# Attention's probabilities times values: native fp32 operands instead of rounded high and low halves

## The chip, the cores and the metric

The kernel runs on one core of a Trainium2 chip. The core has five engines that the text names: TensorE (in the profile PE, with its weight loads as PEld), VectorE (DVE), ScalarE (ACT), GpSimd (POOL) and SyncE (SP), which issues the transfers. Each works through its own queue in the order in which the program was laid out, and waits on semaphores for the others. The metric is the device time of one execution in microseconds (us), lower is better.

## The reference

The reference computes two layers of a diffusion backbone on 512 latent tokens and 256 context tokens of width 1024. Layer 0 mixes tokens by pooling, layer 1 by attention with 8 query heads and 2 key/value heads of width 128; each is followed by an MLP of width 4096 with squared ReLU. The change touches layer 1's attention alone:

```python
def attend(q, k, v):
    s = jnp.einsum('bqhgd,bkhd->bhgqk', q, k).astype(jnp.float32) * (HEAD_DIM ** -0.5)
    p = jax.nn.softmax(s, axis=-1).astype(v.dtype)
    return jnp.einsum('bhgqk,bkhd->bqhgd', p, v)
```

Queries are the 512 latent tokens; keys and values are all 768 tokens. Everything is fp32. The attention output is then multiplied by `w_o` (1024 x 1024).

## The kernel before

**Halves.** Most matmuls take fp32 operands as two rounded halves. ScalarE writes `hi`, the fp32 number rounded to the type that the listing calls `F32R` (fp32r in the profile); VectorE writes `lo = x - hi`, also as fp32r; and TensorE adds three products: hi x hi, hi x lo, lo x hi. A few matmuls (adaLN vectors at L226, gate rows at L302, pooling means at L420) take fp32 operands directly.

**Attention, tile by tile.** A step `i` is a pair (head h, query tile t of 128 tokens); there are 8 x 4 = 32. `s_scores` (L1183) makes 128 x 768 scores with six matmuls (L1191) into one of two large PSUM buffers, VectorE takes the row maximum (L1195), ScalarE the exponential with its row sum (L1196) into a buffer `p` of 768 columns, `pbuf(i % 4)`. `s_norm` (L1200) takes the reciprocal of the row sum (L1202) and scales `p` in place: on VectorE (L1204) in 17 of the steps, on ScalarE (L1206) in 15, by a table written out in the code. `s_turn` (L1208) turns the six 128 x 128 blocks of `p` on TensorE (L1216), three at a time into a PSUM tile `pspt`; ScalarE casts each to the high half (L1218), VectorE subtracts for the low half (L1219). `s_values` (L1221) runs once for two query tiles: for each of six key tiles three matmuls with 128 value columns as weights and 256 queries streaming (L1230), then the output `po` is split into `oH` and `oL` (L1232, L1233). `q_head` (L1175) turns a head's queries (L1179) and splits them.

**Before the attention.** `kv_a` to `kv_c` project keys and values for six token tiles. `kv_e` splits the values into `vH` (L1076) and `vL` (L1077); `kv_b` writes the normalised and rotated keys into a work row `kf`, `kv_c` turns them (L1090). `q_a` projects the queries (L1018) with weight blocks that lie in `unit[0]`, `unit[1]` and `unit[2]`.

**Where things lie.** `unit[1]` and `unit[2]` are two areas of 4096 fp32r columns in one allocation. During the attention the turned probabilities take 3072 columns of each (`pTL`, `pTH`), and the query halves of heads 2 to 7 the rest. Afterwards the second half of the output weights (`wo[1]`) is split into them, in quarters of 512 columns (`split`, L125; L128 and L131).

**Order.** Every piece of work has a time in a list (`st.at`), and the pieces are issued sorted by it; a planner that simulates the program then fixes the order in each engine's queue, save for instructions that are pinned to program order. `attention` (L1271) gives step i its times in units of 2.7 from a base: scores at i + 0.2, scaling at i + 1.3, turning at i + 3.1, values at i + 5.2 for odd t. The output projection (`attn_mm`, L1256) follows in eight blocks; the third is the first that reads `wo[1]`. A tile area that is given back to its pool can be used again when all readers and writers of the old tile are through.

Of the kernel before, what the change touches and what calls it, by code (L numbers as in the profile page):

```python
# [9 lines left out]
F32 = mybir.dt.float32  # L10
F32R = mybir.dt.float32r
BF16 = mybir.dt.bfloat16
AF = mybir.ActivationFunctionType
ALU = mybir.AluOpType
# [3 lines left out]
P = 128  # L18
D = 1024
KT = D // P  # L20
LAT = 512
CTX = 256
TOK = LAT + CTX
NL = LAT // P
NT = TOK // P
# [17 lines left out]
class Steps:  # L43
# [3 lines left out]
    def at(self, t, fn, *args):  # L47
        self.items.append((t, len(self.items), fn, args))
# [7 lines left out]
def backbone(ctx: ExitStack, tc, x, c, ctx_in, c_ctx, w_ada, b_ada, g_mix_pre, g_mix_post,  # L56
# [3 lines left out]
    sy, ve, sc, gp, te = nc.sync, nc.vector, nc.scalar, nc.gpsimd, nc.tensor  # L60
# [3 lines left out]
    rawp = ctx.enter_context(tc.tile_pool(name="rawp", bufs=3, side="right"))  # L64
# [5 lines left out]
    def residents(stack):  # L70
        pool = stack.enter_context(tc.tile_pool(name="residents", bufs=1, side="right"))
        return (pool.tile([P, NT, D], F32, name="xr"), pool.tile([P, 2, D], F32, name="gate"),
                pool.tile([P, D], BF16, name="junk"))

    xr, gate, junk = residents(held[0])
# [4 lines left out]
    acc = const.tile([P, NT * D], F32, name="acc")  # L80
# [9 lines left out]
    ra = const.tile([P, 2 * KT * TOK], F32R, name="ra")  # L90
    rb = const.tile([P, 10240], F32R, name="rb")
    phase = ctx.enter_context(tc.tile_pool(name="phase", bufs=1)).tile([P, 40], F32, name="phase")
    rawe = ExitStack()
    pools = [rawe.enter_context(tc.tile_pool(name="rawe", bufs=4))]
    unit, pinned = [rb[:, 6144:10240]], [True]

    def open_units():
        rawe.close()
        pools[0] = rawp
        units = ctx.enter_context(tc.tile_pool(name="units", bufs=1)).tile([P, 2 * 4096], F32R, name="units")  # L100
        unit.extend(units[:, 4096 * i: 4096 * (i + 1)] for i in range(2))
    minus = phase[:, 0:2 * KT].rearrange("p (k c) -> p k c", c=2)
    hH = ra[:, 0:KT * TOK].rearrange("p (k n) -> p k n", n=TOK)
    hL = ra[:, KT * TOK:].rearrange("p (k n) -> p k n", n=TOK)
# [2 lines left out]
    def raw_load(src, pool=None):  # L107
        t = (pool or pools[0]).tile([P, 2048], F32, tag="raw", name="raw")
        d = sy.dma_start(t, src)
        if pinned[0]:  # L110
            tc.keep_in_program_order(d)
        return t
# [7 lines left out]
    def split_halves(raw, hi, lo, pin=False):  # L120
        for q in range(2):
            z = slice(1024 * q, 1024 * q + 1024)
            split(raw[:, z], hi[:, z], lo[:, z], pin)
# [13 lines left out]
    class Ring:  # L137
# [1 line left out]
            self.slots, self.n, self.halves = slots, 0, halves  # L139

        def load(self, src, width, pin=False, wait=None):
            raw = raw_load(src, rawp)
            s = self.slots[self.n % len(self.slots)]
            self.n += 1
            hi, lo = s[:, 0:2048], s[:, 2048:4096]
            if wait is None and self.halves:
                split_halves(raw, hi, lo, pin)
            elif wait is None:
                split(raw, hi, lo, pin)
            else:  # L150
                wait.append((raw, hi, lo))
            f = lambda a: a.rearrange("p (k n) -> p k n", n=width)
            return f(hi), f(lo)
# [559 lines left out]
    st = Steps()  # L713
# [13 lines left out]
    raws = []  # L727
# [6 lines left out]
    for n, t in enumerate(order):  # L734
        b = 55 + 3 * n
# [9 lines left out]
    for (t, q), z in block.items():  # L745
        st.at(z, turn0, t, q)
        st.at(z + 0.8, mod0, t, q)
        for f in range(2):
            st.at(z + 2.4 if q < 3 else 83 + 2 * f + t / 10, parts0, t, q, f)
    st.at(200, open_units)  # L750
    st.run()

    pso = {}
# [230 lines left out]

    kTH = rb[:, 0:1536].rearrange("p (h n) -> p h n", n=TOK)
    kTL = rb[:, 1536:3072].rearrange("p (h n) -> p h n", n=TOK)
    vH = rb[:, 3072:4608].rearrange("p (t n) -> p t n", n=256)
    vL = rb[:, 4608:6144].rearrange("p (t n) -> p t n", n=256)
    q32 = acc[:, 0:NL * D].rearrange("p (t n) -> p t n", n=D)
    tabs = acc[:, 4 * D:6 * D].rearrange("p (w s t n) -> p w s t n", w=2, s=2, t=NL)  # L990
    swap = lambda a, o: a.rearrange("p (h o d) -> p h o d", o=2, d=32)[:, :, o, :]
# [72 lines left out]
    def norm_g(t, pool=False, cols=HALVES):  # L1064
        yg[t] = work_tile()
        for c0, w in cols:
            z = gated(t, yg[t], accv[:, t, c0:c0 + w], c0, c0 + w, pool)
            if cols == THIRDS:
                tc.keep_in_program_order(z)

    def kv_a(t):
        pj[t] = project(t, chunks[2])

    def kv_e(t):
        ps = pj[t]
        sc.copy(vH[:, t, :], ps[:, 256:512])  # L1076
        ve.tensor_tensor(out=vL[:, t, :], in0=ps[:, 256:512], in1=vH[:, t, :], op=ALU.subtract)  # L1077
        pj[t] = ps, head_rstd(ps, NKV)

    def kv_b(t):  # L1080
        ps, r = pj[t]
        kf = xr[:, 4, 256 * (t % 4):256 * (t % 4) + 256]
        head_norm(ps, r, NKV, 1, t, kf)
        pj[t] = kf

# [59 lines left out]
    def before0():  # L1145
# [8 lines left out]
        for t in (4, 5, 0, 1, 2, 3):  # L1154
# [3 lines left out]

    oH = ra[:, 0:4096].rearrange("p (h n) -> p h n", n=LAT)
    oL = ra[:, 4096:8192].rearrange("p (h n) -> p h n", n=LAT)  # L1160
    qTs = [(z[:, 0:512], z[:, 512:1024]) for z in (unit[0][:, 0:1024], unit[0][:, 1024:2048],
                                                    unit[1][:, 3072:4096], unit[2][:, 3072:4096])]
    qbuf = lambda h: qTs[h if h < 2 else 2 + h % 2]
    pTH = unit[2][:, 0:NT * LAT].rearrange("p (s n) -> p s n", n=LAT)
    pTL = unit[1][:, 0:NT * LAT].rearrange("p (s n) -> p s n", n=LAT)
    pbuf = lambda i: (xr[:, 4, 0:TOK], xr[:, 5, 0:TOK], gate[:, 1, 0:TOK], acc[:, 4 * D:4 * D + TOK])[i]
    aring = Ring([ra[:, 8192:12288], unit[0], unit[1], unit[2]])

    def wo_unit(ch, kk, wait=None):
        return aring.load(w_o[ch, kk], 512, True, wait)  # L1170
# [29 lines left out]
    def s_norm(i):  # L1200
        sm, p = smx[i], pbuf(i % 4)
        ve.reciprocal(sm[:, 2:3], sm[:, 1:2])  # L1202
        if (False,False,False,True,False,True,True,True,True,True,True,True,False,False,True,False,True,False,True,False,True,True,True,False,False,True,False,False,False,False,True,True)[i]:
            ve.tensor_scalar(out=p, in0=p, scalar1=sm[:, 2:3], scalar2=None, op0=ALU.mult)  # L1204
        else:
            sc.activation(p, p, AF.Copy, scale=sm[:, 2:3])  # L1206

    def s_turn(i):  # L1208
        _, t = steps[i]
        sl = slice(t * P, (t + 1) * P)  # L1210
        p = pbuf(i % 4)
        for b in range(2):
            ps = psB.tile([P, 3, P], F32, tag="b", name="pspt")
            for j in range(3):
                k = 3 * b + j
                te.transpose(ps[:, j, :], p[:, k * P:(k + 1) * P], ident)  # L1216
            hi, lo = pTH[:, 3 * b:3 * b + 3, sl], pTL[:, 3 * b:3 * b + 3, sl]
            sc.copy(hi, ps)  # L1218
            ve.tensor_tensor(out=lo, in0=ps, in1=hi, op=ALU.subtract)  # L1219

    def s_values(i):  # L1221
        h, t = steps[i]
        half = t // 2
        kv = h // 4
        hs = slice(kv * HD, (kv + 1) * HD)
        qs = slice(256 * half, 256 * half + 256)
        po = psB.tile([P, 512], F32, tag="b", name="po")
        for kt in range(NT):
            for n, (v, p) in enumerate(((vH, pTH), (vL, pTH), (vH, pTL))):
                te.matmul(po[:, 0:256], v[:, kt, hs], p[:, kt, qs],  # L1230
                          start=(kt == 0 and n == 0), stop=(kt == NT - 1 and n == 2))
        sc.copy(oH[:, h, qs], po[:, 0:256])  # L1232
        ve.tensor_tensor(out=oL[:, h, qs], in0=po[:, 0:256], in1=oH[:, h, qs], op=ALU.subtract)  # L1233

    wo = {0: [], 1: []}
# [35 lines left out]
    def attention(st, base, unit_t):  # L1271
        at = lambda i, fn, *args: st.at(base + unit_t * i, fn, *args)
        for i, (h, t) in enumerate(steps):
            if t == 0:
                at([-2, 3, 4.542, 7.928, 13.236, 15.602, 19.752, 23.755][h], q_head, h)
            at(i + 0.2, s_scores, i)
            at(i + 1.3, s_norm, i)
            at(i + 3.1, s_turn, i)
            if t % 2:
                at(i + 5.2, s_values, i)  # L1280
        raws = []
        at(7, lambda: wo[0].append(wo_unit(0, 0, raws)))
        at(11.386, lambda: wo[0].append(wo_unit(0, 1, raws)))
        for n in range(8):
            at(9.05 + 2 * n, lambda n: split(*raws[n // 4], True, n % 4), n)
        for kk in range(2):
            at((23.386, 25.741)[kk], lambda kk: wo[1].append(wo_unit(1, kk, raws)), kk)
        at(37.812, lambda: split(*raws[2], q=0))
        at(38.427, lambda: split(*raws[2], q=1))
        at(37.814, lambda: split(*raws[2], q=2))  # L1290
        at(37.815, lambda: split(*raws[2], q=3))
        at(39.191, lambda: split(*raws[3], q=0))
        at(39.192, lambda: split(*raws[3], q=1))
        at(39.193, lambda: split(*raws[3], q=2))
        at(45.691, lambda: split(*raws[3], q=3))
        at(39.281, gate_diag if False else gate_rows, 1, GT1, 0)
# [118 lines left out]
```

## Time and profile before

| | us |
|---|---|
| median of three runs (lowest, highest) | 1178.87 (1178.73, 1179.42) |
| the profiled execution's own time | 1180.54 |
| its span, first to last instruction | 1178.7 |
| PE busy in the span | 1142.6 |
| VectorE busy | 941.9 |
| ScalarE busy | 637.5 |
| attention's scores, first matmul to last value matmul | 680.6 to 787.2 |

A group row of the profile reads: line, engine, operation, output and input tiles, shapes and count; then busy time and the mean duration of one in ns; then the engine's idle time just before these instructions and what ended it. A row of the timeline or of the chain begins with the start and the length in us. Durations of matmuls overlap: the spacing of a run of them is its length, less the last one's duration, divided by one less than their count. All profile numbers come from one execution.

### The profile page before, as it was taken

To read this page: it belongs to the slowest core of one execution; us is meant where nothing else is said; L and a number is where in the kernel's file an instruction comes from. 1 tells how busy PE (TensorE), PEld (TensorE's weight loads), DVE (VectorE), ACT (ScalarE), POOL (GpSimd) and SP (SyncE) were. 2 spreads that over 40 slices of the span, in tenths; PEclk is the share of its full clock that TensorE was granted. 3 is DMA by queue.
4 is the path that set the end of the run, shared out by engine and by line. 5 is a ranking of instruction groups with operands and counts; after the bars stand their busy time and mean duration, and the time that the engine had idled before them with its cause. 6 is when DMAs were issued, how large, how long until landed. Compare 5 with 4: busy or idle time off the path is not lost.

```text
span 1178.7 us, 15984 instructions
## 1 busy us (share of the span) xinstructions
PE 1142.6 (97%) x6170; PEld 989.5 (84%) x6170; DVE 941.9 (80%) x1546; ACT 637.5 (54%) x1087; POOL 67.2 (6%) x120
## 2 busy tenths in 40 slices
PE   5899999999999999999999999999899999999997
PEld 4679888989889988998887889998888888888886
DVE  3786778998988999896787689877687779778876
ACT  3666654555354445554676377863676346535522
POOL 2030000000000000000141210001100000000001
PEclk9899999999999999999999999999999999999999
DMA  8974222333334334334422101115234124304312
GB/s 325 369 290 196 72 72 107 143 143 144 143 143 142 113 139 143 107 132 151 182 72 75 70 1 36 37 43 199 110 119 174 48 97 142 108 36 143 107 38 105
DMA packets 25642, 147.84 MB, mean 125 GB/s; under 512 B 2736, under 2 KB 5216, under 8 KB 9824
## 3 DMA queue, kind: packets, MB, share of 16 engines
q1 hardware_dynamic: 25568, 146.84, 34.1%
q8 instruction: 48, 0.79, 0.3%
q14 instruction: 26, 0.21, 0.1%
HBM read 139.49 MB, written 7.34 MB: 125 GB/s over the span
## 4 chain that ended last, share of the span: by engine, by line
PE 54%; issue 33%; DVE 5%; ACT 3%; POOL 3%; DMA 1%; SPq 0%; POOLq 0%; DVEq 0%; ACTq 0%
PE pso L771 22%; PE psin L677 18%; PE psin L553 3%; PE po L1230 2%; PE psy L1256 2%; PE psq L1018 2%; PE pss L1191 2%; POOL rs L171 1%; PE psada L226 1%; PE psm L420 1%; POOL rs L1027 1%; ACT junk L156 1%; DVE sm L1195 1%; PE pspt L1216 1%; DVE units L1219 1%
## 5 line engine op out<-in xcount | busy, mean ns | idle before, releaser
L771 PE MATMUL pso<-units,rb 128*128 128x512 f32 x1152 | 278.9, 392 | 0.0
L771 PEld LDWEIGHTS pso<-units,rb 128*128 128x128 f32 x1152 | 214.7, 188 | 41.1
L268 DVE SCALAR_TENSOR_TENSOR rows<-raw,cond,rows 128x256 f32<-128x256 f32 x280 | 127.1, 479 | 2.0
L783 DVE TENSOR_TENSOR acc<-acc,pso 128x512 f32<-128x512 f32 x129 | 85.4, 677 | 41.8 <-PE pso L771 41.7
L553 PE MATMUL psin<-ra,rb 128*128 128x512 f32 (+1 forms) x432 | 104.8, 342 | 2.4 <-ACT ra L363 1.6
L875 PE MATMUL pso<-units,pairs 128*128 128x512 f32 x336 | 82.3, 389 | 0.0
L553 PEld LDWEIGHTS psin<-ra,rb 128*128 128x128 f32 x432 | 70.3, 189 | 13.7 <-ACT ra L363 1.9
L553 PE MATMUL psin<-ra 128*128 128x512 f32 x256 | 80.5, 389 | 0.0
L875 PEld LDWEIGHTS pso<-units,pairs 128*128 128x128 f32 x336 | 63.1, 188 | 13.1
L879 DVE TENSOR_TENSOR acc<-acc,pso 128x512 f32<-128x512 f32 x72 | 48.8, 683 | 28.6 <-PE pso L875 28.6
L169 POOL TENSOR_SCALAR ms<-ss 128x1 f32<-128x1 f32 x20 | 11.0, 549 | 1000.7 <-ACT junk L156 989.2
L677 PE MATMUL psin<-ra,units 128*128 128x384 f32 x336 | 65.5, 337 | 0.4 <-ACT psin L689 0.4
L677 PE MATMUL psin<-sums,units 128*128 128x384 f32 x336 | 64.0, 336 | 0.0
L677 PEld LDWEIGHTS psin<-ra,units 128*128 128x128 f32 x336 | 59.8, 188 | 3.9 <-ACT psin L689 0.5
L131 DVE TENSOR_TENSOR units<-raw,units 128x1024 fp32r<-128x1024 f32 (+2 forms) x49 | 55.2, 1153 | 6.5 <-ACT units L128 6.3
L677 PEld LDWEIGHTS psin<-sums,units 128*128 128x128 f32 x336 | 58.9, 188 | 1.6
L128 ACT CAST units<-raw 128x1024 fp32r<-128x1024 f32 (+2 forms) x49 | 46.9, 995 | 17.7 <-PE pso L771 13.7
L553 PEld LDWEIGHTS psin<-ra 128*128 128x128 f32 x256 | 48.1, 188 | 10.0
L781 ACT COPY acc<-pso 128x512 f32<-128x512 f32 x48 | 27.1, 587 | 48.2 <-PE pso L771 47.7
L553 PE MATMUL psin<-rb 128*128 128x512 f32 (+1 forms) x144 | 52.8, 367 | 0.2 <-DVE rb L364 0.2
L1018 PE MATMUL psq<-units,ra 128*128 128x512 f32 x216 | 51.7, 392 | 0.0
L553 PE MATMUL psin<-rb,ra 128*128 128x512 f32 x128 | 49.8, 389 | 0.0
(255 smaller groups left out, 2355.7 us busy)
## 6 DMA issues: line engine op xcount, KB each, us to landing
raw<-in_w_ada SPq DMA_DIRECT2D x48, 1024.0 KB, 4.9
raw<-in_w_mlp_in SPq DMA_DIRECT2D x32, 1024.0 KB, 4.8
raw<-in_w_mlp_out SPq DMA_DIRECT2D x32, 1024.0 KB, 5.0
raw<-in_w_qkv SPq DMA_DIRECT2D x6, 1024.0 KB, 4.8
spill<-xr SPq DMA_DIRECT2D x10, 512.0 KB, 9.1
xr<-spill SPq DMA_DIRECT2D x10, 512.0 KB, 5.6
raw<-in_w_o SPq DMA_DIRECT2D x4, 1024.0 KB, 4.9
xr<-in_x SPq DMA_DIRECT2D x4, 512.0 KB, 4.4
```

The costliest lines, as they stand in the source:

```text
L128: a = sc.copy(hi, raw)
L131: b = ve.tensor_tensor(out=lo, in0=raw, in1=hi, op=ALU.subtract)
L268: ve.scalar_tensor_tensor(out=r, in0=raw[:, k, :], scalar=cond[:, k, c:c + 1], in1=r, op0=ALU.mult, op1=ALU.add)
L553: te.matmul(ps[:, bank, o:o + ln], w[:, k, fs], rhs, start=start, stop=(k == KT - 1 and n == 2), skip_group_check=len(ks) < KT)
L677: te.matmul(bank, w[k], a[k], start=start and k == 0 and m == 0, stop=stop and k == 3 and m == 2, skip_group_check=True)
L771: te.matmul(pss[h][:, 0:cols[h][1]], a[:, f, ts_], w[:, f, cols[h][0]:sum(cols[h])], start=(n == 0 and not seeded[t]), stop=(n == len(seq) ...
L781: sc.copy(d, ps)
L783: ve.tensor_tensor(out=d, in0=d, in1=ps[:, 0:w], op=ALU.add)
L875: te.matmul(ps, a, w, start=(m == 0), stop=(m == len(seq) - 1))
L879: ve.tensor_tensor(out=M[n][:, t], in0=M[n][:, t], in1=ps, op=ALU.add)
L1018: te.matmul(ps, a[:, k, sl], w[:, k % 4, :], start=(k == 0 and n == 0), stop=(k == KT - 1 and n == 2))
L1191: te.matmul(ps[:, c2, 0:384], a[:, sl], b[:, kv, 384 * c2:384 * c2 + 384], start=(n == 0), stop=(n == 2))
```

## The change

- `s_values` multiplies fp32 probabilities by fp32 values: one matmul per key tile instead of three.
- The turned probabilities are copied once, as fp32 (`soft["t"]`), and the values are copied once, as fp32 (`values()`, in the rows 4 and 5 of `xr`, which are free by then); L1077 and L1219 are gone.
- The keys' work row `kf` has two places instead of four.
- All 32 scalings are on VectorE.
- `unit[1]` and `unit[2]` are given up at the start of the attention (`open_soft`) for fp32 tiles: query halves of heads 2 to 7, turned probabilities, two of the four `p` buffers. At the end (`close_soft`) the two units are opened again. The second half of `w_o` is loaded at the same steps as before, but gets its place in a unit after that.

```diff
     def open_units():
-        rawe.close()
-        pools[0] = rawp
-        units = ctx.enter_context(tc.tile_pool(name="units", bufs=1)).tile([P, 2 * 4096], F32R, name="units")
-        unit.extend(units[:, 4096 * i: 4096 * (i + 1)] for i in range(2))
+        units = uheld[0].enter_context(tc.tile_pool(name="units", bufs=1)).tile([P, 2 * 4096], F32R, name="units")
+        unit[1:] = [units[:, 4096 * i: 4096 * (i + 1)] for i in range(2)]
...
+    values = lambda: xr[:, 4:6].rearrange("p t n -> p (t n)")[:, 0:1536].rearrange("p (t n) -> p t n", n=256)
...
-        sc.copy(vH[:, t, :], ps[:, 256:512])
-        ve.tensor_tensor(out=vL[:, t, :], in0=ps[:, 256:512], in1=vH[:, t, :], op=ALU.subtract)
+        sc.copy(values()[:, t, :], ps[:, 256:512])
...
-        kf = xr[:, 4, 256 * (t % 4):256 * (t % 4) + 256]
+        kf = xr[:, 5, 512 + 256 * (t % 2):768 + 256 * (t % 2)]
...
-    pbuf = lambda i: (xr[:, 4, 0:TOK], xr[:, 5, 0:TOK], gate[:, 1, 0:TOK], acc[:, 4 * D:4 * D + TOK])[i]
-    aring = Ring([ra[:, 8192:12288], unit[0], unit[1], unit[2]])
+    aring = Ring([ra[:, 8192:12288], unit[0], None, None])
+    soft = {}
+
+    def open_soft():
+        uheld[0].close()
+        pool = uheld[0].enter_context(tc.tile_pool(name="soft", bufs=1))
+        qs = pool.tile([P, 2 * 1024], F32R, name="qs")
+        qTs.extend((qs[:, 1024 * i:1024 * i + 512], qs[:, 1024 * i + 512:1024 * i + 1024]) for i in range(2))
+        soft["t"] = pool.tile([P, NT, LAT], F32, name="pT")
+        ps = [pool.tile([P, TOK], F32, name=f"p{i}") for i in range(2)]
+        soft["p"] = ps
+
+    def close_soft():
+        uheld[0].close()
+        open_units()
+        aring.slots[2:] = unit[1:]
+
+    pbuf = lambda i: soft["p"][i - 1] if i in (1, 2) else (gate[:, 1, 0:TOK], acc[:, 4 * D:4 * D + TOK])[i // 2]
...
-        if (False,False,False,True,False,True,True,True,True,True,True,True,False,False,True,False,True,False,True,False,True,True,True,False,False,True,False,False,False,False,True,True)[i]:
-            ve.tensor_scalar(out=p, in0=p, scalar1=sm[:, 2:3], scalar2=None, op0=ALU.mult)
-        else:
-            sc.activation(p, p, AF.Copy, scale=sm[:, 2:3])
+        ve.tensor_scalar(out=p, in0=p, scalar1=sm[:, 2:3], scalar2=None, op0=ALU.mult)
...
-            hi, lo = pTH[:, 3 * b:3 * b + 3, sl], pTL[:, 3 * b:3 * b + 3, sl]
-            sc.copy(hi, ps)
-            ve.tensor_tensor(out=lo, in0=ps, in1=hi, op=ALU.subtract)
+            sc.copy(soft["t"][:, 3 * b:3 * b + 3, sl], ps)
...
-            for n, (v, p) in enumerate(((vH, pTH), (vL, pTH), (vH, pTL))):
-                te.matmul(po[:, 0:256], v[:, kt, hs], p[:, kt, qs],
-                          start=(kt == 0 and n == 0), stop=(kt == NT - 1 and n == 2))
+            te.matmul(po[:, 0:256], values()[:, kt, hs], soft["t"][:, kt, qs], start=(kt == 0), stop=(kt == NT - 1))
...
-        raws = []
+        raws, late = [], []
+        at(1.1, open_soft)
+        at(37.5, close_soft)
...
-            at((23.386, 25.741)[kk], lambda kk: wo[1].append(wo_unit(1, kk, raws)), kk)
+            at((23.386, 25.741)[kk], lambda kk: late.append(raw_load(w_o[1, kk], rawp)), kk)
+            at(37.6, lambda kk: wo[1].append(aring.place(late[kk], 512, raws)), kk)
```

More of the change, by code (lines that the diff above doesn't have):

```diff
@@ L94, in backbone @@
     pools = [rawe.enter_context(tc.tile_pool(name="rawe", bufs=4))]
-    unit, pinned = [rb[:, 6144:10240]], [True]
+    unit, pinned, uheld = [rb[:, 6144:10240]], [True], [ctx.enter_context(ExitStack())]
     def open_units():
-        rawe.close()
-        pools[0] = rawp
-        units = ctx.enter_context(tc.tile_pool(name="units", bufs=1)).tile([P, 2 * 4096], F32R, name="units")
-        unit.extend(units[:, 4096 * i: 4096 * (i + 1)] for i in range(2))
+        units = uheld[0].enter_context(tc.tile_pool(name="units", bufs=1)).tile([P, 2 * 4096], F32R, name="units")
+        unit[1:] = [units[:, 4096 * i: 4096 * (i + 1)] for i in range(2)]
     minus = phase[:, 0:2 * KT].rearrange("p (k c) -> p k c", c=2)
@@ L141, in load, with place @@
         def load(self, src, width, pin=False, wait=None):
-            raw = raw_load(src, rawp)
+            return self.place(raw_load(src, rawp), width, wait, pin)
+        def place(self, raw, width, wait=None, pin=False):
             s = self.slots[self.n % len(self.slots)]
@@ L749, in backbone, with end_loads @@
             st.at(z + 2.4 if q < 3 else 83 + 2 * f + t / 10, parts0, t, q, f)
-    st.at(200, open_units)
+    def end_loads():
+        rawe.close()
+        pools[0] = rawp
+        open_units()
+    st.at(200, end_loads)
     st.run()
@@ L986, in backbone @@
     kTL = rb[:, 1536:3072].rearrange("p (h n) -> p h n", n=TOK)
-    vH = rb[:, 3072:4608].rearrange("p (t n) -> p t n", n=256)
-    vL = rb[:, 4608:6144].rearrange("p (t n) -> p t n", n=256)
     q32 = acc[:, 0:NL * D].rearrange("p (t n) -> p t n", n=D)
@@ L1160, in backbone @@
     oL = ra[:, 4096:8192].rearrange("p (h n) -> p h n", n=LAT)
-    qTs = [(z[:, 0:512], z[:, 512:1024]) for z in (unit[0][:, 0:1024], unit[0][:, 1024:2048],
-                                                    unit[1][:, 3072:4096], unit[2][:, 3072:4096])]
+    qTs = [(z[:, 0:512], z[:, 512:1024]) for z in (unit[0][:, 0:1024], unit[0][:, 1024:2048])]
     qbuf = lambda h: qTs[h if h < 2 else 2 + h % 2]
-    pTH = unit[2][:, 0:NT * LAT].rearrange("p (s n) -> p s n", n=LAT)
-    pTL = unit[1][:, 0:NT * LAT].rearrange("p (s n) -> p s n", n=LAT)
-    pbuf = lambda i: (xr[:, 4, 0:TOK], xr[:, 5, 0:TOK], gate[:, 1, 0:TOK], acc[:, 4 * D:4 * D + TOK])[i]
-    aring = Ring([ra[:, 8192:12288], unit[0], unit[1], unit[2]])
+    aring = Ring([ra[:, 8192:12288], unit[0], None, None])
[10 more added lines that the diff above has]
+        uheld[0].close()
+        open_units()
+        aring.slots[2:] = unit[1:]
+    pbuf = lambda i: soft["p"][i - 1] if i in (1, 2) else (gate[:, 1, 0:TOK], acc[:, 4 * D:4 * D + TOK])[i // 2]
     def wo_unit(ch, kk, wait=None):
```

## The prediction

> **What bounds the kernel now.** I read the page first, to see which engine fills the span.
>
> ```profile
> span 1178.7 us, 15984 instructions
> PE 1142.6 (97%) x6170; PEld 989.5 (84%) x6170; DVE 941.9 (80%) x1546; ACT 637.5 (54%) x1087; POOL 67.2 (6%) x120
> ```
>
> TensorE (PE) is busy for 97% of the span, but the edit lies almost wholly in the attention stage. So I cut that stage out next, by windows (columns: stretch, its length, then busy time and instruction count of PE, weight loads, VectorE, ScalarE, GpSimd).
>
> ```profile
> 687.00:700.00 13.00, 11.24 (x71) 9.70 (x69) 11.56 (x24) 10.31 (x27) 1.20 (x2) 1.00 0.00 1
> 700.00:775.00 75.00, 72.47 (x539) 70.14 (x538) 68.11 (x139) 64.19 (x139) 0.00 (x0) 1.00 0.08 29
> 775.00:790.00 15.00, 14.48 (x113) 13.42 (x113) 10.55 (x24) 10.09 (x24) 0.00 (x0) 1.00 0.01 3
> ```
>
> Three engines are nearly level here: of 103 us PE is busy 98.2, VectorE 90.2, ScalarE 84.6. PE leads, but it does stop for the others. How tight it is packed is read from the chain of waits in order of time, where PE runs without a break:
>
> ```profile
> 744.76 1.31 PE pss L1191 x6
> 746.08 0.33 PE pspt L1216 x3
> 746.41 2.15 PE po L1230 x18
> 748.56 0.66 PE pspt L1216 x6
> 749.21 1.06 PE pss L1191 x6
> ```
>
> and from the groups by line between 687 and 790 us, which give the counts:
>
> ```profile
> L1230 PE MATMUL po<-units,rb 128*128 128x256 f32 x288 | 38.1, 286 | 2.1 <-DVE sm L1202 1.1 <-DVE units L1219 0.9
> L1219 DVE TENSOR_TENSOR units<-pspt,units 128x384 fp32r<-128x384 f32 x64 | 33.6, 549 | 0.2
> L1191 PE MATMUL pss<-rb,units 128*128 128x384 f32 x144 | 31.6, 351 | 0.9 <-ACT xr L1196 0.8
> L1216 PE MATMUL pspt<-ident,xr 128*128 128x128 f32 x96 | 14.3, 274 | 0.1
> L1191 PE MATMUL pss<-rb 128*128 128x384 f32 x42 | 8.8, 347 | 1.5 <-ACT acc L1196 0.9 <-ACT gate L1196 0.4
> L1206 ACT ACTIVATE xr<-xr,sm 128x768 f32<-128x768 f32 x8 | 7.6, 950 | 0.0
> L1216 PE MATMUL pspt<-ident,gate 128*128 128x128 f32 x48 | 7.4, 273 | 0.3 <-DVE units L1219 0.3
> L1216 PE MATMUL pspt<-ident,acc 128*128 128x128 f32 x48 | 6.9, 273 | 0.0
> L1204 DVE TENSOR_SCALAR xr<-xr,sm 128x768 f32<-128x768 f32 x7 | 4.3, 614 | 0.1
> L1179 PE MATMUL pq<-ident,acc 128*128 128x128 f32 x28 | 4.2, 272 | 0.0
> ```
>
> At unbroken rates PE needs 186/6 = 31 score groups x 1.06 = 32.9 us, 192/6 = 32 transposed tiles x 0.66 = 21.1, 288/18 = 16 value calls x 2.15 = 34.4 and 28 query transposes x 0.11 (0.66/6) = 3.1: 91.5 us. The stage takes 100.2 us, from 687.0 to the last value matmul's end near 787.2 (row below). So 8.7 us are slack: part is the 4.8 us in which PE is not busy in the windows, the rest lies in short pauses that the busy time of pipelined matmuls covers. The sum below sets what the change adds to the 91.5 against what it takes from the 8.7.
>
> **The change, part by part.**
>
> *Values in native fp32 (the main term).* A call goes from 18 matmuls on rounded halves to 6 on fp32. The nearest rows of native fp32, and rows of the rounded kind with 512 columns, from the timeline and the groups by line (19 to 98 us):
>
> ```profile
> 787.07 1.72 PE L302 MATMUL psg<-ident,gc 128*128 128x128 f32 x14
> 791.39 2.88 PE L1256 MATMUL psy<-rb,ra 128*128 128x512 f32 x12
> 794.11 2.88 PE L1256 MATMUL psy<-ra 128*128 128x512 f32 x12
> L226 PE MATMUL psada<-raw,cond 128*32 128x512 f32 x96 | 12.8, 637 | 0.0
> L226 PE MATMUL psada<-raw,cond 128*32 128x256 f32 x128 | 10.0, 417 | 0.9 <-ACT work L452 0.7 <-DVE acc L390 0.2
> L302 PE MATMUL psg<-ident,gc 128*128 128x128 f32 x32 | 4.0, 277 | 0.6 <-DVE gc L291 0.6
> ```
>
> First, native fp32 runs as two records: the code calls the matmul of L302 16 times in this window (four half rows of four), the row shows 32; L226 likewise has 112 calls and 224 records. So a value call becomes 12 records. Second, each record streams at half rate: L226 costs 637 - 417 = 220 ns for 256 more columns, 0.86 ns a column, while the rounded kind goes from 2.15/18 = 0.119 us at 256 columns to (794.11 - 791.39)/12 = 0.227 at 512, 0.42 ns a column. No row has a 256-column native record with 128 stationary columns. Bounds: L302 at 128 columns is spaced (1.72 - 0.277)/13 = 0.111 us; 128 more columns at twice 0.42 give 0.218, and the 512-column rounded row, as much streaming with a heavier fixed part, gives 0.227. I take 0.222, between two close ends. A call: 12 x 0.222 = 2.66 against 2.15; 16 calls: **+8.2 us** (+7.5 to +9.1), all on PE's queue.
>
> The Trainium skill says the same of the passes ("FP8 and Floating Point Precision", TensorE Precision Notes: "True FP32: 4 passes through PE array"). With the 2.4 GHz of its page "TensorE: Matmul & The Clock Gate" (What's actually happening), an estimate is 6 x 4 x 256 columns = 2.56 us a call, +6.6 us, against +8.2 from the rows, which hold each record's fixed part too.
>
> *Low halves of the probabilities go (L1219).* 64 x 0.549 = 35.1 us leave VectorE. *All scalings on VectorE (L1203).* L1206 runs 14 times after 687 us and once before; 15 x 0.95 = 14.2 us leave ScalarE and 15 x 0.614 = 9.2 us arrive on VectorE. VectorE falls from 90.2 to some 65 us, ScalarE from 84.6 to 71, PE rises to 99.7 of pure work. Neither takes PE's place. What they give is time on PE: shorter queues in front of the exponentials, which free the score banks (the releasers named in the L1191 rows), and of the casts (L1202 and L1219, named in the L1230 row). In the first 13 us (groups by line, 687 to 700 us)
>
> ```profile
> L1219 DVE TENSOR_TENSOR units<-pspt,units 128x384 fp32r<-128x384 f32 x6 | 3.2, 548 | 0.0
> L1206 ACT ACTIVATE xr<-xr,sm 128x768 f32<-128x768 f32 x1 | 1.0, 974 | 0.0
> L1206 ACT ACTIVATE gate<-gate,sm 128x768 f32<-128x768 f32 x1 | 0.9, 938 | 0.5 <-DVE sm L1202 0.5
> ```
>
> 6 low halves (3.3 us) go from VectorE but 2 scalings (1.2 us) come, and the stage has only begun to fill, so the 1.76 us of idle PE shrink in part. In the steady 75 us PE becomes longest by far, and most pauses should fill. I take half of the slack, 4.4 us, as recovered: **-4.3 us**; bounds 0 (the same order stalls as before) and -8.7 (none is left).
>
> *Low half of the values (L1077).*
>
> ```profile
> L1077 DVE TENSOR_TENSOR rb<-psq,rb 128x256 fp32r<-128x256 f32 x6 | 2.5, 420 | 2.8 <-ACT rb L1076 2.8
> 630.00:680.00 50.00, 49.70 (x224) 40.77 (x225) 33.40 (x58) 20.91 (x73) 11.49 (x18) 1.00 0.23 85
> ```
>
> 2.5 us leave VectorE around 617 to 646 us, where PE is busy 49.70 of 50: 0, at best -0.3. *Keys' work rows in two buffers instead of four.* The third tile's write now waits for the first tile's transposes:
>
> ```profile
> 623.01 0.38 PE L1090 MATMUL pk<-ident,xr 128*128 128x128 f32 x2
> 631.63 0.42 DVE L1048 TENSOR_TENSOR xr<-work 128x256 f32<-128x256 f32 x1
> ```
>
> They are 8 us apart: 0.
>
> *Units closed and reopened.* At the front the fp32 buffers take the place of the units that the last query projection reads, so the exponential of step 1 must now wait for that projection. Queued behind it on ScalarE are the casts of the first transposed tile, and PE's next transposes wait for their banks. At the back, the quarters of the last output weights (8 casts, 8 low halves) may be written only once every reader of the fp32 buffers is through.
>
> ```profile
> 681.66 5.64 PE L1018 MATMUL psq<-units,ra 128*128 128x512 f32 x24
> 689.40 0.90 ACT L1196 ACTIVATE xr<-pss,sm 128x768 f32<-128x768 f32 x1 [0.43 <-DVE sm L1195]
> 785.17 4.26 ACT L128 CAST units<-raw 128x512 fp32r<-128x512 f32 x8
> 786.16 1.08 PE L1230 MATMUL po<-units,rb 128*128 128x256 f32 x7
> 791.35 0.68 DVE L131 TENSOR_TENSOR units<-raw,units 128x512 fp32r<-128x512 f32 x1
> 799.55 0.62 PE L1256 MATMUL psy<-units,ra 128*128 128x512 f32 x2
> ```
>
> The projection ends at 687.3, the exponential starts at 689.40: 2.1 us of cover, 0 (to +1 if the order changes). The casts move from 785.17 to after 787.2, 2 us later, and the last low half from 792.0 to 794, while the first reader starts at 799.55, after four blocks of projection that use other weights: 5 us of cover, 0 (to +2 if the static order also puts the gate copies and evictions behind them). The loads of these weights are issued at the same steps as before, on the same queue: 0.
>
> **Sum.** +8.2 - 4.3 = +3.9 us. The profiled execution has a span of 1178.7 us, its own time is 1180.54; the median of the runs is 1178.87, so I put the sum on the median: **1182.8 us**. Limits of the same sum: +7.5 - 8.7 = -1.2 gives 1177.7; +9.1 + 0 gives 1188.0.
>
> **Rivals.**
>
> *A. The slack goes wholly (no change).* The added PE work then merely fills the pauses: -0.5 with the middle price, 1178.4; it holds from a recovery of 5.9 us upwards (8.2 - 5.9 = 2.3). For it: three engines are level now and two drop by 13 and 25 us. Against: the first 13 and the last 12 us are chains through one tile, which no lighter engine removes.
>
> *B. Weight loads are what PE is paced by (faster).* Weight loads are busy for 70.14 of the steady 75 us. If each record cost its load's spacing, 0.119 us, whatever it streams, 12 instead of 18 would make a call 1.43 us: -0.72 x 16 = -11.5, 1167.4; with the 4.3 us above, it decides faster once a native record costs less than 0.189 us (16 x (12 x 0.189 - 2.15) - 4.3 = -2.4). Against it: with the same load, records of 256, 384 and 512 columns are spaced 0.119, 0.177 (1.06/6) and 0.227, so the streaming sets the pace. The Trainium skill ("Perfetto Trace Analysis", Identifying the Most-Contended Engine) advises judging TensorE by the share of LDWEIGHTS rather than by matmul busy time; by that reading this stage would gain, and these rows speak against it.
>
> *C. The order written by the planner gets worse (much slower).* The step times were set for the old balance. If PE's fixed order puts value calls ahead of late casts, slack grows rather than shrinks; one pause of 0.6 us more in front of each value call, half of the 1.1 us that the L1230 row names, is 16 x 0.6 = +9.6 on top of +8.2: 1196.7. Against: with ScalarE and VectorE lighter, casts come earlier.
>
> *D. A reopened buffer waits.* +2 to +3 over the sum: 1185.3, part of the forecast's side.
>
> **Chances.** The forecast (slower by up to 9 us, D in it) 0.56; A 0.25; B, or full recovery with a native record at its cheapest and a quicker front, 0.15; C 0.04. From no change 0.2% (2.4 us) can be told. So slower 0.60, within 0.24, faster 0.16. The range reaches from 1176 (just beyond the sum's lower limit) to 1189 (its upper limit and a little of D): it leaves out most of B and C. The forecast's own range is 1181.3 to 1188.
>
> **What would show it.** L1230: 192 records of 128x256 spaced 0.22 us, no low halves, no L1206; the stage to the last value matmul some 104 us; VectorE near 65 us busy in it; PE never idle for long after 700 us. It is wrong if the native record costs under 0.2 or over 0.24 us, if the pauses in front of scores stay, if the exponential of step 1 starts later than 2.1 us after the last projection, or if the output projection on the reopened units waits for its weights.

## The result and the profile after

The changed kernel takes 1181.22 us (median of 22 runs) against 1179.43 us for the kernel before on the same chips (22 runs): ratio 1.0015, 95% interval 1.0009 to 1.0021. It is slower by about 1.8 us, clear of noise, yet below the 0.2% that the prediction took as its bound for "no change". The profiled execution after has a shorter span than the one before (1178.3 against 1178.7 us). That is no gain: in it the first adaLN matmul starts at 17.5 us instead of 19.2, before anything that was changed, and all later work is earlier by that.

So the stage is measured by itself, from the end of the last query projection (687.3 us before, 685.3 after) to the end of the last value matmul. The view is one window of exactly that length, with the columns of the prediction's windows; the last three are the granted clock, the DMA share and the GB/s. Before:

```profile
687.30:787.20 99.90, 95.10 (x699) 90.43 (x698) 87.37 (x179) 81.80 (x182) 1.20 (x2) 1.00 0.06 22
```

After:

```profile
685.30:786.90 101.60, 99.60 (x604) 92.03 (x604) 69.45 (x129) 71.36 (x165) 1.20 (x2) 1.00 0.06 22
```

The stage grew by 1.7 us, about the whole difference. PE is now busy for 99.6 of its 101.6 us; VectorE fell from 87.4 to 69.5, ScalarE from 81.8 to 71.4. The groups by line of the kernel after (685 to 788 us), then the row of ScalarE's casts in the kernel before (687 to 788 us), then one value call of the timeline after:

```profile
L1241 PE MATMUL po<-pT,xr 128*128 128x256 f32 x192 | 44.1, 379 | 0.0
L1208 PE MATMUL pss<-rb,qs 128*128 128x384 f32 x144 | 31.4, 351 | 0.0
L1208 PE MATMUL pss<-rb 128*128 128x384 f32 x42 | 8.9, 350 | 2.0 <-ACT acc L1213 1.6 <-ACT p L1213 0.4
L1231 ACT COPY pT<-pspt 128x384 f32<-128x384 f32 x64 | 28.5, 481 | 11.0 <-PE pspt L1230 10.8
```

```profile
L1218 ACT CAST units<-pspt 128x384 fp32r<-128x384 f32 x64 | 28.8, 489 | 6.1 <-PE pspt L1216 5.7
```

```profile
772.01 2.76 PE L1241 MATMUL po<-pT,xr 128*128 128x256 f32 x12
```

The native calls show 192 records, 12 a call, spaced (2.76 - 0.379)/11 = 0.216 us: 2.59 us a call against 2.15. PE no longer waits for anybody in front of value calls (0.0), and in front of scores only at the front of the stage. ScalarE waits more for PE: 10.8 us in front of the copies, 5.7 before.

With the prediction's unbroken rates PE needs 91.5 us before and 31 x 1.06 + 21.1 + 16 x 2.59 + 3.1 = 98.5 us after. (A few gate matmuls of L302, 0.2 to 0.6 us, lie in the stage as well and are not in these sums.) What is left of the stage is its slack: 99.9 - 91.5 = 8.4 us before, 101.6 - 98.5 = 3.1 after. The price is 7.0 us, 5.3 us of slack were recovered.

The two ends of the reopened buffers, in the timeline after:

```profile
679.65 5.64 PE L1021 MATMUL psq<-units,ra 128*128 128x512 f32 x24
687.39 0.90 ACT L1213 ACTIVATE p<-pss,sm 128x768 f32<-128x768 f32 x1 [0.41 <-DVE sm L1212]
787.16 3.74 ACT L126 CAST units<-raw 128x512 fp32r<-128x512 f32 x7
787.81 4.91 DVE L129 TENSOR_TENSOR units<-raw,units 128x512 fp32r<-128x512 f32 x8
798.95 0.61 PE L1266 MATMUL psy<-units,ra 128*128 128x512 f32 x2
```

The exponential of step 1 still starts 2.1 us after the projection's end (685.3), and it is VectorE's row maximum that it waits for. The casts of the last weights do move behind the last value matmul (786.9), and the last low half is done at 792.7, 6 us before its reader.

### The profile page after: what moved, and what is told of

Same layout as the page of the kernel before. It is cut to its first block, busy times and chain, and to the rows that moved or that the text cites. A ratio compares the mean times of both kernels' runs of the same rounds, so it can differ in the third digit from the quotient of the medians.

```text
span 1178.3 us, 15759 instructions
## 1 busy us (share of the span) xinstructions
PE 1145.3 (97%) x6074; PEld 990.0 (84%) x6074; DVE 922.6 (78%) x1491; ACT 627.6 (53%) x1072; POOL 68.8 (6%) x120
## 4 chain that ended last, share of the span: by engine, by line
PE 48%; issue 43%; DVE 4%; POOL 2%; ACT 2%; DMA 1%; SPq 0%; POOLq 0%; DVEq 0%; ACTq 0%
PE pso L776 22%; PE psin L677 18%; PE psq L1021 3%; PE psin L553 3%; POOL rs L171 1%; PE psada L226 1%; POOL rs L1030 1%; ACT junk L156 1%; PE psm L420 1%; PE pspool L480 1%; DVE xr L328 1%; POOL ms L169 0%; DMA xr<-in_ctx 0%; DMA xr<-in_x 0%; DVE rows L268 0%
## 5 line engine op out<-in xcount | busy, mean ns | idle before, releaser
L786 ACT COPY acc<-pso 128x512 f32<-128x512 f32 x48 | 27.1, 586 | 48.3 <-PE pso L776 47.8
```

The lines of the kernel that those rows point to most:

```text
L786: sc.copy(d, ps)
```

## The experiments

Each stage below runs from the end of the last query projection to the end of the last value matmul, as above; the slack is the stage less PE's work (91.5 us with rounded calls, 98.5 with native ones). Each stage length comes from one execution. The medians of the runs bear them out: where the stages of experiments 1, 2, 4 and 5 move by -3.5, +6.4, +3.9 and -5.6 us, the times move by -2.6, +6.3, +4.1 and -5.0.

**1. The relief without the price.** The kernel before, all scalings on VectorE, low halves for the first head only (8 of the 64 stay; the later heads multiply by them, so PE's work is the same):

```diff
-        if (False,False,False,True,...)[i]:
+        ve.tensor_scalar(out=p, in0=p, scalar1=sm[:, 2:3], scalar2=None, op0=ALU.mult)
...
-            ve.tensor_tensor(out=lo, in0=ps, in1=hi, op=ALU.subtract)
+            if i < 4:
+                ve.tensor_tensor(out=lo, in0=ps, in1=hi, op=ALU.subtract)
```

> The kernel before, with the relief alone: all scalings on VectorE, and the low half of the turned probabilities made for the first head only (steps 0 to 3; the later heads multiply by that stale low half, so the output lacks their own low products). TensorE still runs 18 matmuls a value call. Theory 1 (slack is filled because VectorE and ScalarE got lighter): the stage from the end of the last query projection to the end of the last value matmul falls from 99.9 us by 4.4 to 5.5 us, and the time by as much, 0.4 to 0.5%. Rival 2 (the slack went because the longer value call itself covers the others; lighter engines alone do nothing): 0 to -1 us.

```profile
686.60:783.00 96.40, 92.75 (x697) 90.21 (x696) 71.73 (x138) 72.23 (x168) 1.20 (x2) 1.00 0.07 23
```

Ratio 0.9978 (0.9968 to 0.9989); the stage fell by 3.5 us, slack 4.9. Lighter engines alone fill slack, so the second theory falls; but the gain is below the 4.4 to 5.5 that the first expected.

**2. The price without the relief.** The changed kernel with the low half still subtracted, into a scratch tile that nobody reads, and the old scaling table:

```diff
-            sc.copy(soft["t"][:, 3 * b:3 * b + 3, sl], ps)
+            hi = soft["t"][:, 3 * b:3 * b + 3, sl]
+            sc.copy(hi, ps)
+            ve.tensor_tensor(out=soft["d"], in0=ps, in1=hi, op=ALU.subtract)
...
```

> The changed kernel with the load of the others as before: the low half is still subtracted on VectorE, into a scratch tile that nobody reads, and the scalings follow the old table. Native fp32 value calls stay. Theory 1: the price of 16 x (12 x 0.216 - 2.15) = 7.1 us is paid with little of the slack recovered: +5 to +7 us against the kernel before (0.4 to 0.6%). Rival 2 (the longer call covers the others by itself): +2 us, as the changed kernel.

```profile
686.30:792.60 106.30, 102.00 (x601) 91.93 (x600) 88.47 (x178) 80.42 (x178) 1.20 (x2) 1.00 0.06 21
```

Ratio 1.0053 (1.0037 to 1.0070); the stage is 6.4 us longer than before and the slack 7.8 us, nearly the 8.4 of the kernel before. PE's waits in that stage are mostly for exponentials (ACT L1214) in front of scores. The longest ones, first of the kernel before, then of this one:

```profile
PE po L1230 <- DVE sm L1202: 1.1, 1, 1.1
PE pss L1191 <- ACT acc L1196: 0.9, 1, 0.9
PE po L1230 <- DVE units L1219: 0.9, 2, 0.4
```

```profile
PE pss L1209 <- ACT p L1214: 1.6, 2, 1.1
PE pss L1209 <- ACT acc L1214: 0.9, 1, 0.9
PE pspt L1234 <- DVE ra L1249: 0.7, 1, 0.7
```

The waits in front of value calls (L1230) are gone and others have come in their place. With the others as loaded as they were, native calls cost almost their full price.

**3. The scalings undone in the changed kernel** (the old table is put back, nothing else).

> The changed kernel with the scalings shared between VectorE and ScalarE as before (15 on ScalarE). Theory 1: TensorE stays the longest engine (VectorE some 56 us, ScalarE some 85 of 101), so +0 to +1 us against the changed kernel, +1.8 to +2.8 us against the kernel before. Rival 3 (it is the moved scalings that paid): +4 to +6 us against the kernel before.

```profile
685.40:785.90 100.50, 99.74 (x604) 91.89 (x604) 61.33 (x114) 80.28 (x178) 1.20 (x2) 1.00 0.06 22
```

Ratio to the kernel before 1.0005 (0.9995 to 1.0016). The stage is 1.1 us shorter than that of the changed kernel, not longer. This kernel differs from the one of experiment 2 by the low halves alone: leaving them out is worth 106.3 - 100.5 = 5.8 us, and moving the scalings to VectorE then loses 1.1 us of it. In experiment 2 nobody reads the low half, so its cost is not a value call waiting for it; whether it is VectorE's time, or the bank of the turned tile that is held until the subtraction, these runs do not separate.

**4. The scalings alone, in the kernel before.**

> The kernel before with all scalings on VectorE and nothing else changed. Theory 1: VectorE goes from 90 to some 99 us of the stage and becomes its longest engine: +4 to +9 us against the kernel before (0.3 to 0.8%). Rival 3 (the moved scalings pay by themselves): -1 to -4 us.

```profile
686.40:790.20 103.80, 95.08 (x698) 90.62 (x697) 94.61 (x194) 71.62 (x169) 1.20 (x2) 1.00 0.06 21
```

```profile
PE pss L1191 <- ACT xr L1196: 4.1, 5, 1.7
PE pss L1191 <- ACT acc L1196: 1.6, 1, 1.6
```

Ratio 1.0035 (1.0022 to 1.0048): +3.9 us of stage. VectorE, at 94.6 us, is now as busy as PE. PE waits in front of scores for exponentials; that these are late because VectorE's row maximum is late is the reading of its load, no run of its own. The third rival, that the moved scalings pay, falls in both kernels.

**5. Relief with the old table** (experiment 1 with the table kept).

> The kernel before without the low half of the turned probabilities after the first head (the later heads use the stale one, so their own low products are left out), and with the old scaling table. In the run with relief alone the stage fell 3.5 us although its first value call came 4 us later than before, behind two pauses of 1.6 us in front of scores, which the all-VectorE scalings make while rotary work still fills VectorE. If that is so, the table gives these pauses back: stage 94 to 95.5 us, -4.5 to -6 us against the kernel before. If the scalings cost nothing: 96.4 us as in that run.

```profile
689.80:784.10 94.30, 92.53 (x696) 89.86 (x695) 63.67 (x123) 81.80 (x182) 1.20 (x2) 1.00 0.07 23
```

Ratio 0.9958 (0.9943 to 0.9972). The stage is 5.6 us shorter than before, and the slack 2.8 us. The low halves are worth about the same with rounded calls (5.6 us for 56 of them) as with native ones (5.8 for 64); what experiment 1 missed is the 2.1 us that its scalings cost.

**6. The fourth buffer.** Steps 3, 7, ... use the keys' rotary table, free by then, instead of the queries' one:

```diff
-(gate[:, 1, 0:TOK], acc[:, 4 * D:4 * D + TOK])[i // 2]
+(gate[:, 1, 0:TOK], acc[:, 5 * D:5 * D + TOK])[i // 2]
```

> The changed kernel with the buffer of every fourth step (3, 7, ...) moved from the queries' rotary table, which the last query tile still reads, to the keys' table, which is free by then. In the changed kernel TensorE stands 1.6 us in front of the scores of step 5, because the exponential of step 3 waits for the last rotary product. If that wait is what is left of the slack at the front: the stage falls from 101.6 to 100 us, -1.0 to -1.7 us against the changed kernel, within 0.5 us of the kernel before. If another tile of the filling pipeline takes its place: 0 to -0.4 us.

> The same move of that buffer in the kernel before, where TensorE stands 0.9 us at the same place: -0.5 to -1.1 us against the kernel before if that wait counts; 0 if VectorE, full in these 13 us, is late anyway.

The changed kernel with this: ratio 1.0013 (1.0003 to 1.0022), stage 101.2 us, -0.4. The kernel before with it: 0.9995 (0.9986 to 1.0005), stage 99.5 us, -0.4. In front of the scores of step 5 the pause shrinks but does not go. The timeline, first of the changed kernel, then of that kernel with the move:

```profile
694.18 0.98 PE L1208 MATMUL pss<-rb 128*128 128x384 f32 x4 [1.57 <-ACT acc L1213]
```

```profile
695.09 1.31 PE L1208 MATMUL pss<-rb 128*128 128x384 f32 x6 [0.70 <-ACT acc L1213]
698.44 0.84 PE L1230 MATMUL pspt<-ident,acc 128*128 128x128 f32 x6 [0.29 <-DVE sm L1219]
```

The last row shows another tile late in its place. So the wait was not what was left of the slack (1.0 to 1.7 us), and the other expectation (0 to 0.4 us) holds for the changed kernel; in the kernel before, the 0.4 us lie between its two expectations. The likely reading is that at the front the pipeline is filling and several of its steps are late at once.

**7. Where the scalings cost.** Only steps 0 to 4 on ScalarE, in the changed kernel.

> The changed kernel with the scalings of steps 0 to 4 on ScalarE and all later ones on VectorE. If the 1.0 us that the whole table gave comes from the front, where VectorE is full: stage 100.2 to 100.8 us, first value call 11.5 us after the projection's end instead of 12.4. If it comes from the steady part: 101.6 us as the changed kernel.

Ratio to the kernel before 1.0006 (0.9997 to 1.0015), stage 101.1 us, between the two expectations: about half of the 1.1 us came back. Where the cost lies is read from the first value call, in the kernel before, the changed one, experiment 3 and this one:

```profile
699.94 2.40 PE L1230 MATMUL po<-units,rb 128*128 128x256 f32 x18
697.73 2.76 PE L1241 MATMUL po<-pT,xr 128*128 128x256 f32 x12
696.93 2.76 PE L1244 MATMUL po<-pT,xr 128*128 128x256 f32 x12
698.20 2.76 PE L1244 MATMUL po<-pT,xr 128*128 128x256 f32 x12
```

Ahead of it PE has 36 score matmuls, 24 transposes of probabilities and 8 of queries: 6 x 1.06 + 4 x 0.66 + 8 x 0.11 = 9.9 us (12.0 in experiments 1 and 4, where two score groups more come first). That splits the slack of each stage in two (us):

| | first value call after the projection's end | slack ahead of it | slack behind it |
|---|---|---|---|
| before | 12.6 | 2.7 | 5.7 |
| before, scalings on VectorE (4) | 16.5 | 4.5 | 7.8 |
| before, no low halves, scalings on VectorE (1) | 16.5 | 4.5 | 0.4 |
| before, no low halves (5) | 12.6 | 2.7 | 0.1 |
| changed | 12.4 | 2.5 | 0.6 |
| changed, load as before (2) | 12.6 | 2.7 | 5.1 |
| changed, old table (3) | 11.5 | 1.6 | 0.4 |
| changed, steps 0 to 4 on ScalarE (7) | 12.0 | 2.1 | 0.5 |

The low halves make nearly all of the slack behind the first value call. Ahead of it they are worth 1.1 us (2.7 against 1.6 in experiments 2 and 3; experiment 5 keeps those of the first head, and its front is as before), and there the scalings of the changed kernel take 0.9 us of that back. So nearly all of their cost lies at the front. Moving steps 0 to 4 gives back half of it; the old table leaves step 3 on VectorE, but no run changes that step alone, so why the rest did not come back is not shown.

**8. Mixtures.** Query tiles 0 and 1 of a head go through native calls, 2 and 3 through three products of halves, with both kinds of values kept and the fourth buffer as in 6; scalings all on VectorE, by the old table, or with steps 0 to 4 on ScalarE:

```diff
+            if half == 0:
+                te.matmul(po[:, 0:256], values()[:, kt, hs], soft["t"][:, kt, :], start=(kt == 0), stop=(kt == NT - 1))
+                continue
+            for n, (v, p) in enumerate(((vH, soft["h"]), (vL, soft["h"]), (vH, soft["l"]))):
...
```

> A mixture: query tiles 0 and 1 of a head go through native fp32 value calls, tiles 2 and 3 through three products of halves (fp32 and rounded values are both kept), all scalings on VectorE, the fourth buffer as in the run before. If the price is 0.44 us a native call and the slack is set by how much lighter VectorE is: half the price (8 x 0.44 = 3.5 us) and half of the low halves back on VectorE (+17.6 us, near 87 of 98): stage 98 to 99.5 us, -0.5 to -2 us against the kernel before. If VectorE at that load stalls TensorE as it did before: 0 to +2 us.

> The same mixture with the scalings shared by the old table (15 on ScalarE): VectorE near 78, ScalarE near 81 of 98 us. The table gave the changed kernel -1.0 us of stage; with TensorE the longest by more than 10 us over both: stage 96.5 to 98 us, -2 to -3.5 us against the kernel before (0.17 to 0.3%). If halves and full values at the front (one more copy and subtraction for each of six token tiles) delay the queries: -0.5 to -2 us.

> The mixture of native calls (tiles 0, 1) and halves (tiles 2, 3) with the scalings of steps 0 to 4 on ScalarE. If front pauses are what the mixture still loses: stage 97.0 to 97.7 us against 98.0 with all scalings on VectorE, -2.2 to -2.9 us against the kernel before. If the table as a whole hurts the mixture (98.6 us) for its front part: 98 to 98.6 us.

```profile
687.20:785.20 98.00, 96.54 (x650) 90.99 (x650) 81.34 (x161) 70.13 (x164) 1.20 (x2) 1.00 0.06 23
```

The row is the first mixture's. The stages are 98.0, 98.6 and 98.4 us, 1.3 to 1.9 us shorter than before, but the times cannot be told from it: ratios 0.9997 (0.9987 to 1.0007), 0.9993 (0.9984 to 1.0003), 0.9997 (0.9989 to 1.0006). About 1 us is given back ahead of the stage: from the first key/value projection to the last query projection's end it is 83.5 us in the mixtures against 82.5 before, with a copy more for each of six token tiles. Neither the full table nor ScalarE at the front helped the mixture's stage, against the first expectation of each. No kernel here that computes all products is clearly faster than the kernel before.

## Why the prediction was right, and where it was off

The range held the time, the direction was right, and the chain of reasons stands in the main: the cost is on PE, and part of it is paid from slack that VectorE had caused. That the range held says little, since its 13 us (1176 to 1189) also hold no change and a gain; the forecast's own range began at 1181.3, just above the measured 1181.22. Point by point:

- **Price of the native calls.** Two records per matmul, each at half rate, 192 in all, as said. Their spacing is 0.216 us, below even the lower of the two bounds (0.218). The step that failed is the choice of 0.222 between the bounds: the native records carry less fixed time than the rounded ones. 256 columns at twice the prediction's 0.42 ns are 215 ns, so 0.216 leaves about 1 ns; by the two native rows alone (0.111 us at 128 columns, 0.216 at 256) 128 columns take 105 ns and 6 are left. The rounded 256-column record, 108 ns of columns in 119, leaves 11. The term is +7.0 us, not +8.2. The estimate of +6.6 worked out with the Trainium skill's pages "FP8 and Floating Point Precision" (TensorE Precision Notes) and "TensorE: Matmul & The Clock Gate" was the nearer one.
- **Recovered slack.** Taken as half, 4.4 of 8.7 us; measured 5.3 of 8.4. Experiment 2 shows that the longer call absorbs 0.6 us by itself, experiments 3 and 5 that the low halves give 5.6 to 5.8. The half was an average of two stretches that behave differently: behind the first value call nearly all of the slack went (5.7 to 0.6 us), ahead of it almost nothing (2.7 to 2.5), since the scalings took back most of what the low halves gave there. So one sign of being wrong came in part: the pauses in front of scores went in the steady part (0.9 us to 0.0) and stayed at the front (1.5 in the prediction's row, 2.0 after). Nor did it need a lighter ScalarE: with the old table ScalarE is nearly as busy as before (80.3 us against 81.8) and the slack behind the first value call is 0.4 us.
- **VectorE's relief.** It fell to 69.5 us busy, not to some 65. The 64 low halves are worth 88.47 - 61.33 = 27.1 us of busy time (experiments 2 and 3) and not the sum of their durations, 35.1: neighbouring instructions overlap. Two scalings of 0.62 and 0.61 us, for example, start at 695.16 and 695.69 us in the timeline after, 0.53 us apart.
- **All scalings on VectorE.** The prediction booked this together with the low halves as relief. That was wrong in sign: it costs 1.1 us in the changed kernel (experiment 3), 2.1 us in experiment 1 against 5, and 3.9 us in the kernel before (experiment 4). By the table of experiment 7 it is 1.8 us ahead of the first value call where low halves are still made there (experiments 1 and 4), and 0.9 where they are not; behind it the scalings cost 2.1 us where VectorE is as busy as PE, and at most 0.3 where it is lighter. That the recovery still came out near the half is partly luck: the low halves gave more, and the scalings took some back.
- **The sum.** +6.4 (native calls, others as loaded as before) - 5.8 (low halves) + 1.1 (scalings) = +1.7 us of stage. The three terms are differences of measured stages, so they must close on the 1.7 of the window; the medians, 1.8, are the independent check. The forecast of +3.9 was too large by 1.2 us of price and about 1 us of slack.
- **Steps costed at nothing.** The stretch of projections ahead of the stage went from 82.5 to 82.2 us: the values' low half gave the 0.3 us named as its best case. Both waits of the reopened units stayed hidden, with 2.1 and 6 us to spare.
- **Rivals.** A (no change) came nearest: the recovery of 5.3 us is just short of the 5.9 it asked for. Behind the first value call the slack did go nearly wholly, and the front that it named against itself is where slack stayed. B falls: with the same 128x128 load a native record is spaced 0.111 us at 128 columns and 0.216 at 256, so its columns set the pace. The loads' busy time even rose, from 90.4 to 92.0 us, with 94 fewer records. The Trainium skill's advice to judge TensorE by that share beside the MFU ("Perfetto Trace Analysis", Identifying the Most-Contended Engine) would not, by the share alone, have ranked these two kernels: both stages show 91% of loads, while PE's slack fell from 8.4 to 3.1 us. The MFU is not taken here. C did not happen (0.0 us of waiting in front of value calls). D cost nothing.
- **Chances.** Slower by over 0.2% had 0.60, within 0.2% had 0.24. With a measured 0.15% the smaller one happened, because the price was put 1.2 us too high and the recovery 1.0 us too low.

## What to carry to other kernels

Where three engines are level, the cost of an operation on the longest one and the relief of the two others must be priced apart: here +6.4 and -5.8 us nearly cancel, and a third term that was booked as relief, the scalings moved to another engine, is 1.1 of the 1.7 us that are left. The slack, too, is better counted by stretches: what a lighter engine recovers behind the filling of the pipeline it need not recover in it. One run that keeps the price and one that keeps the relief are enough to see it. In a stage that PE paces, the useful number is PE's work at unbroken rates against the stage's length, since busy shares of a pipelined engine hide the short pauses.

## What the runs showed beyond that

**Native fp32 has little fixed time per record.** It is spaced 0.216 us at 256 columns, 1 to 6 ns over its streaming by the two readings above. In the value call of this kernel native fp32 costs 20% more PE time than three rounded products (2.59 against 2.15), and it saves one VectorE pass for each turned tile.

**After one pause the clock is halved in some executions.** At the start of layer 1's MLP, near 840 us, TensorE has about 5 us with only twelve transposes. In 4 of the 13 profiled executions the matmuls behind it then ran at a granted clock of 0.50 for 3.4 us. The stretch from the first output projection to the last matmul took 384.7 us in these and 383.1 to 383.2 in the others. Windows of the same work, first the changed kernel, then that of experiment 6 and the slow stretch within it, with the granted clock in the third column from the end:

```profile
841.00:849.00 8.00, 5.54 (x43) 5.09 (x44) 5.89 (x10) 6.81 (x10) 0.00 (x0) 1.00 0.00 0
```

```profile
842.40:850.40 8.00, 5.53 (x31) 5.08 (x32) 5.90 (x10) 6.80 (x10) 0.00 (x0) 0.80 0.00 0
847.20:850.60 3.40, 3.40 (x18) 3.40 (x18) 2.54 (x4) 3.23 (x3) 0.00 (x0) 0.50 0.00 0
```

The order of the work and its waits are the same in both; 12 fewer matmuls fit into the same 8 us. The Trainium skill says why it may differ ("TensorE: Matmul & The Clock Gate", What's actually happening): the window that watches activity runs freely and is not tied to the kernel's start. The runs agree with that, but none here moves the pause against the window, and each of the 13 kernels was profiled once, so that chance and not the kernel decides is not shown. The difference of 1.5 us is nearly as large as the effect studied, and it is one reason to compare stages and not only times.
